# A hybrid attention and RWKV-7 layer on one Trainium2 core: scores in quarters of the array, a chain over two PSUM banks, a product that moves, and groups that start later

## Chip, core and metric

One core of a Trainium2 chip runs the whole layer in one launch. The metric is the device time of an execution in microseconds (us). Engines: TensorE (PE; its weight loads are listed as PEld), VectorE (DVE), ScalarE (ACT), GpSimd (POOL), SyncE (SP, which issues most DMAs). Each engine runs its own instructions in the order in which they were issued to it.

## The reference

`x` is 512 tokens of 1024 features, all fp32. 16 meta tokens are put ahead, so T = 528. After a layer norm, one product with `w_in` (1024 x 6656) gives everything that the two mixers need:

```python
q, k, v        # sliding-window attention: 16 query heads of 64, 2 key/value heads,
               # window 128, T5 relative bias, one sink a head
r, k, v, wl, al, gl = split(token_shift(z, mu))          # RWKV-7: 16 heads of 64
w = -softplus(-(w0 + tanh(wl) @ w2)) - 0.5;  decay = exp(-exp(w))
a = sigmoid(a0 + al @ a2);  g = sigmoid(gl) @ g2
kk = normalize(k * k_k);    k = k * (1 + (a - 1) * k_a)

def step(S, inp):                                        # S: 64 x 64 a head, T steps
    r_t, w_t, k_t, v_t, kk_t, a_t = inp
    sa = einsum('bhij,bhj->bhi', S, -kk_t)
    S = S * w_t + sa (x) (kk_t * a_t) + v_t (x) k_t      # outer products
    return S, einsum('bhij,bhj->bhi', S, r_t)

y = group_norm(y) * lnx_g + lnx_b
y = (y + sum(r * k * r_k) * v) * g                       # per head
```

The two results are merged by sigmoid gates, go through `w_out`, a residual and a layer norm, and then through an MLP of 4096 with squared ReLU and a second residual and norm.

## The kernel before

**Products in three.** An fp32 product is made of three matmuls on halves (`three`, L340 to L342): high by high, high by low, low by high. Weights arrive by DMA as `wraw` (128 x 1024, 512 KB), ACT casts the high half (`whi`, L256), DVE subtracts to get the low half (`wlo`, L259), one pair of instructions for each 512 columns. `hhi` and `hlo` are the halves of the normalized input, features on partitions. A *dense unit* is one 128-column tile of `w_in`: eight k steps of three matmuls, over two spans of 264 tokens (form 128x264) or, for queries and gates, one of 512 (128x512), into one of two banks `dps`.

**RWKV-7 in chunks.** The 16 heads go in 8 pairs, 128 partitions a pair, head 0 in rows 0 to 63 and head 1 in rows 64 to 127 (`ER`). The 512 tokens are 8 chunks of 64. For a pair:

- `rwkv_begin` and `rwkv_lora` (`llo`, L499; ACT `ta`, L500) make the decays. The evictions of the keys' unit (`k`) and the reads' unit (`r`) make the scaled vectors `BK` and `AX`; `rwkv_sums` takes norms (`ss`), DVE inverts them (`dv`). `rwkv_reads` runs when `r` is ready. It fills `AX` and then makes the product `rk` = r k r_k (L594), its high half `rkh` (ACT, L599) and low half `rkl` (DVE, L600).
- `rwkv_scores` (i = 0 and 1, four chunks each) multiplies `BK` (64 rows a head, 128 columns, one half for each kind of key) with `AX` (128 columns): eight matmuls `sc` (L668) a half, 64 rows by 128 columns, one bank a head. In a head's bank, the head's own 64 rows hold one kind of product, and the other 64 rows the other. Six DVE instructions take them out: `NT` (L676) twice and `GR` (L681) twice from the own rows, `AX` (L685) twice from the other rows.
- `rwkv_bonus` sums `rkh` and `rkl` over a head and multiplies with `v`; the result `bv` goes to memory and comes back as `bvm` for the output.
- The chunk's triangular matrix is inverted (`XB`, `X` L841, `up` L846, L822), then `rwkv_fold` (`wp` L873, `gq` L890) folds it into `AX`.
- `rwkv_chain` carries the state through the chunks in seven steps. A step is two matmuls `ch` (L948), head 0 into rows 0 to 63 and head 1 into rows 64 to 127 of one bank, eight steps side by side in it; then `follow` scales head 0's half on DVE (L906) and head 1's on ACT (L908) into `Z`, which the next step reads.
- `rwkv_outputs` (`Y`, L962), sums of squares (`grs`, with a power on POOL), `gyn`, `rwkv_norm`, then `z` (L1209, L1210), the gate, and the merge.

**Attention.** A query unit's eviction writes `qhi` (ACT, L1071) and `qlo` (DVE, L1072); four DMAs on SP (L1081) copy their halves to `qs0` and `qs1`, one tile a head. `qhi` lies in the tile with tag `sph`, of which there is one. `attention_scores` makes `sp` (L1136) in four parts, then `sb`, probabilities, transposes (`pt`, `pown`) and the outputs `o`. `turn_heads` (L1046) transposes the value heads (`vp`, L1052); it runs once for each of the two value heads.

**PSUM** has eight banks: two for `dps`, two with tag `g` (`sc`, `axt`, `gq`, `wp`, `bp`, `up`), two with tag `a` (`sp`, `vp`, `gp`, the lora's products, `ss`), one `ch` and one `Y`.

**What sets the order.** PE's order is written out by hand. The program goes through ten stages, s = -1 to 8. Stage s holds the inversion and chain of pair s - 1 (`solve`), the scores of pair s (`scan`), lora and norms of pair s + 1 (`project_in`), attention of pair s - 1, and the outputs and joins of pairs before. `weave` walks through a stage's list of steps, each with a start time, and puts k steps of the dense units between them until the sum of their estimated times reaches that start. The units of a stage come in this order: the RWKV gate and the attention gate of s - 1, the keys and reads of s + 1, the query of s, the values of s + 1. The instructions of the other engines come from the same functions; a scheduler sets their order by priorities (`PRI`), and the engines then run it in order. DMAs that SP issues stand in one queue in SP's order; weights are asked for two tiles ahead (L350).

The lines around the starts of the steps:

```python
            if s in (1, 5):
                items += [(8.6, (), turn_heads)]
            if 0 < s < PAIRS - 1:
                items += attend(s - 1, 9.2) + join(s - 1, 11.6, 25.4, 0)[:2]
```

Of the kernel before, what the change touches and what calls it, by code (L numbers as in the profile page):

```python
# [11 lines left out]
F32 = mybir.dt.float32  # L12
# [8 lines left out]
P = 128  # L21
# [7 lines left out]
HD = 64  # L29
# [101 lines left out]
def hybrid_layer_kernel(ctx: ExitStack, tc: tile.TileContext, I: dict, out: bass.AP):  # L131
# [454 lines left out]
    def rwkv_reads(j, r):  # L586
        S = SS[j]
        AXg = S["AX"].rearrange("p c k e t -> p e c k t")
        rx = c64(r)
        for e in range(2):  # L590
            R = slice(e * HD, (e + 1) * HD)
            dve.tensor_tensor(AXg[R, e, :, 1, :], rx[R], S["Px"][R, :, 1:], op=ALU.mult)
        rk = ew.tile([P, SEQ], F32, name="rk", tag="rk")
        dve.scalar_tensor_tensor(  # L594
            rk, r[:, NMETA:], vcol("r_k", j), S["kp"][:, NMETA:], op0=ALU.mult, op1=ALU.mult
        )
        rkh = ew.tile([P, SEQ], F32R, name="rkh", tag="rkh")
        rkl = ew.tile([P, SEQ], F32R, name="rkl", tag="u")
        act.copy(rkh, rk)  # L599
        dve.tensor_tensor(rkl, rk, rkh.bitcast(F32), op=ALU.subtract)  # L600
        S["rk"] = rkh, rkl
# [52 lines left out]
    def rwkv_scores(j, i):  # L654
        S = SS[j]
        if i == 0:
            S["NT"] = rw.tile([P, NCH, C], F32, name="NT", tag="NT", bufs=NBUF["NT"])
            S["GR"] = rw.tile([P, NCH, P], F32, name="GR", tag="GR", bufs=NBUF["GR"])
            S["Nd"] = dr.tile([BLKS], F32, name=f"Nd{j}")
        BK, dv, NT, GR, Nd = S["BK"], S["dv"], S["NT"], S["GR"], S["Nd"]  # L660
        AXg = S["AX"].rearrange("p c k e t -> p e c k t")
        msc = cv("msc")
        cs = slice(4 * i, 4 * i + 4)
        scs = [pg.tile([P, 512], F32, name="sc", tag="g") for e in range(2)]

        for c in range(4):
            for e in range(2):
                pe.matmul(  # L668
                    scs[e][:, c * P : (c + 1) * P], BK[ER[e], 4 * i + c, :],
                    AXg[ER[e], e, 4 * i + c], start=True, stop=True,  # L670
                )
        q4 = [ps.rearrange("p (c t) -> p c t", c=4) for ps in scs]
        with ahead(PRI["scores"]):
            for e in range(2):
                R = ER[e]
                dve.tensor_tensor(  # L676
                    NT[R, cs, :], q4[e][R, :, 0:C], B64(dv[R, cs], C), op=ALU.mult
                )
            for e in range(2):
                R, K_ = ER[e], ER[1 - e]  # L680
                dve.tensor_tensor(  # L681
                    GR[R, cs, C:P], q4[e][R, :, C:P],
                    msc[R, C:P].unsqueeze(1).to_broadcast([HD, 4, C]), op=ALU.mult,
                )
                dve.tensor_tensor(  # L685
                    AXg[K_, e, cs], q4[e][K_].rearrange("p c (k t) -> p c k t", k=2),
                    msc[K_].rearrange("p (k t) -> p k t", k=2).unsqueeze(1).to_broadcast(
                        [HD, 4, 2, C]
                    ), op=ALU.mult,
                )  # L690
        if i == 1:
            for e in range(2):
                nc.sync.dma_start(
                    blocks(Nd, 4 * e * BSTEP, [C, C], [8 * BSTEP, NCH], [1, C]), NT[ER[e]]
                )
# [204 lines left out]
    def follow(S, c, src, last):  # L900

        Z, PC = S["Z"], S["PC"]
        for e in range(2):
            dst, scale = Z[c][ER[e], e, :], PC[ER[e], last : last + 1]
            if e == 0:
                dve.tensor_scalar(dst, src[ER[e]], scale, None, op0=ALU.mult)  # L906
            else:
                act.activation(dst, src[ER[e]], AF.Copy, scale=scale)  # L908

    def rwkv_start(j, n):  # L910

        S = SS[j]
        if n == 0:
            S["meta"] = pch.tile([P, 512], F32, name="meta", tag="ch", bufs=PS[2])
            S["RHm"] = rw.tile([NMETA, 2, HD], F32, name="RHm", tag="RHm", bufs=2)
        ps, RHm = S["meta"], S["RHm"]
        p6 = [ps[:, q * C : (q + 1) * C] for q in range(6)]
        m = slice(0, NMETA)
        with ahead(PRI["start"]):
            if n == 0:  # L920
                for e in range(2):
                    pe.matmul(
                        p6[e][m], S["AKm"][:, e, :], S["SVm"][:, e, :], start=True, stop=True
                    )
                act.copy(RHm.rearrange("p e i -> p (e i)"), ps[m, 0 : 2 * C])
            if n == 1:
                for e in range(2):
                    pe.matmul(p6[2 + e][m], S["XTm"][:, e, :], RHm[:, e, :], start=True, stop=True)
                for e in range(2):
                    act.copy(S["SVm"][32 * e : 32 * e + NMETA, e, :], p6[2 + e][m])  # L930
            if n == 2:
                for e in range(2):
                    pe.matmul(
                        p6[4][ER[e]], S["BTm"][:, e, :], S["SVm"][:, e, :], start=True, stop=True
                    )
                follow(S, 0, p6[4], NCH)

    def rwkv_chain(j, c):

        S = SS[j]  # L940
        Z, GQ = S["Z"], S["AX"]
        if c == 0:
            ch = pch.tile([P, 512], F32, name="ch", tag="ch", bufs=PS[2])
            S["st"] = [ch[:, d * C : (d + 1) * C] for d in range(NCH)]
        st = S["st"]
        with ahead(PRI["chain"]):
            for e in range(2):
                pe.matmul(st[c][ER[e]], GQ[:, c, 0, e, :], Z[c][:, e, :], start=True, stop=True)  # L948
            follow(S, c + 1, st[c], c)

    def rwkv_outputs(j):
# [433 lines left out]
    def scan(j):  # L1385

        need = (f"k{j}", f"r{j}", f"v{j}")
        return [
            (0.0, need, F(rwkv_scores, j, 0)),
            (3.2, (), F(rwkv_meta, j)),  # L1390
            (3.2, (), F(rwkv_scores, j, 1)),
            (3.2, (), F(rwkv_inverse, j)),
            (5.6, (), F(rwkv_bonus, j)),
            (12.4, (), F(rwkv_turn_scores, j)),
            (18.6, (), F(rwkv_turn_keys, j)),
            (16.0, (), F(rwkv_inverse_place, j)),
            (23.2, (), F(rwkv_turn_values, j)),
        ]
# [45 lines left out]
    with tc.manual_schedule(engines={mybir.EngineType.PE}):  # L1444
        for s in range(-1, PAIRS + 1):
            if s <= PAIRS:
                units[:] = [u for u in all_units[: marks[s + 1]] if u[0] not in finished]
            items = []
            if s > 0:
                items += solve(s - 1)  # L1450
            if 0 <= s < PAIRS:
                items += scan(s)
            if s == -1:
                items += [
                    (0.0, (), F(rwkv_begin, 0)),
                    (9.0, ("wa",), F(rwkv_lora, 0, 0)),
                    (10.4, (), F(rwkv_lora, 0, 1)),
                    (20.0, ("k0",), F(rwkv_sums, 0)),
                ]
            if 0 <= s < PAIRS - 1:  # L1460
                items += project_in(s + 1)
            if s == 0:
                items += [(18.0, ("av",), F(aside_heads, 0))]
            if s == 4:
                items += [(26.0, (), F(aside_heads, 1))]
            if s in (1, 5):
                items += [(8.6, (), turn_heads)]
            if 0 < s < PAIRS - 1:
                items += attend(s - 1, 9.2) + join(s - 1, 11.6, 25.4, 0)[:2]
            if 1 < s < PAIRS:  # L1470

                items += attend_out(s - 2, 0.0, 4.6, 6.4) + join(s - 2, 0, 0, 7.0)[2:]
            if s == PAIRS - 1:
                items += [(10.0, (), merged_before)]
                items += attend(s - 1, 10.0) + attend_out(s - 1, 20.5, 22.9, 25.3)
                items += join(s - 1, 11.6, 26.5, 26.5)
                items += attend(s, 16.5)
                items += [(27.2, (), F(load_out, q, 0)) for q in range(3)]
            if s == PAIRS:
                items += attend_out(s - 1, 3.0, 5.4, 7.8) + join(s - 1, 0.0, 24.5, 25.5)  # L1480
                items += [(2.0, (), F(merged, s - 2)), (25.6, (), F(merged, s - 1))]
                items += [(3.0, (), residual_gain), (17.0, (), first_up)]
                items += [(3.0 + 3 * b, (), F(residual_rows, b)) for b in range(4)]
            weave(items, True)
# [262 lines left out]
```

## Time and profile before

| | us |
|---|---|
| median of 3 runs | 985.71 (983.71 to 985.78) |
| profiled execution, its own time | 984.06 |
| its span, first to last instruction | 982.3 |
| granted TensorE clock over the span | 0.997 of full |
| one inner stage, 165.0 to 228.5 | 63.5 |

"Busy" is the time in which an engine worked on an instruction, over the span. A row of a list of waits reads: engine, tile and line that waited, the engine, tile and line that it waited for, then the total in us, how often, and the longest. A timeline row reads: start, duration, engine, line, operation, tile written and tiles read, shapes, the count of like rows drawn together, and in brackets the idle time before it and what ended it. In a list of DMAs the last number is the median from issue to landing. An order row, further on, has no time: it is the line, the operation, output and inputs, and the shape.

### The profile page before, as it was taken

Reading aid. Unit: us, or ns where it says so; the run is one execution under the profiler, and the core shown is the slowest. Engines: PE = TensorE matmul, PEld = TensorE weight load, DVE = VectorE, ACT = ScalarE, POOL = GpSimd, SP = SyncE. Lnnn points to the kernel's source line nnn. Section 1 sums busy time; section 2 is a strip of 40 time slices with the busy share of each in tenths; the row PEclk is TensorE's granted clock in tenths of the full one; section 3 lists DMA queues with packets and bytes.
Section 4 is the critical chain, followed back from the end, with each engine's and each line's share of the span. In section 5 each row is a group of like instructions: output and inputs, shape, how many; then the busy total and the mean of one; then the engine's idle time right before and its main releaser. Section 6 shows DMA issues by size and latency. Waiting matters only on the chain.

```text
span 982.3 us, 19147 instructions
## 1 busy us (share of the span) xinstructions
PE 940.8 (96%) x7557; PEld 787.7 (80%) x7557; DVE 655.2 (67%) x1505; ACT 455.7 (46%) x1130; POOL 47.8 (5%) x108
## 2 busy tenths in 40 slices
PE   4989999999999999999998999999999999999996
PEld 3889878788887887887876778988888888888885
DVE  8677888877977788778876957566423244452427
ACT  6636457465474654745736724644321133432220
POOL 2001000010000100100001001000000000000001
PEclk9999999999999999999999999999999999999998
DMA  7546323223333332242434635133322323222222
GB/s 273 95 130 166 86 75 103 79 71 109 87 91 100 104 98 79 65 111 78 144 108 105 206 119 214 44 129 107 104 89 91 103 87 107 86 95 98 79 94 85
DMA packets 82674, 105.47 MB, mean 107 GB/s; under 512 B 47766, under 2 KB 54664, under 8 KB 82584
## 3 DMA queue, kind: packets, MB, share of 16 engines
q1 hardware_dynamic: 81088, 102.16, 34.3%
q10 hardware_dynamic: 1496, 2.08, 0.6%
q8 instruction: 59, 0.97, 0.4%
q14 instruction: 31, 0.25, 0.1%
HBM read 86.29 MB, written 13.74 MB: 102 GB/s over the span
## 4 chain that ended last, share of the span: by engine, by line
PE 72%; DVE 17%; ACT 4%; DMA 2%; issue 2%; POOL 2%; SPq 0%; DVEq 0%; ACTq 0%
PE dps L340 12%; PE dps L341 11%; PE dps L342 11%; PE acc L1516 6%; PE acc L1518 6%; PE acc L1517 6%; DVE wlo L259 3%; PE sc L668 2%; PE o L1290 1%; PE av L1194 1%; PE ch L948 1%; PE wp L873 1%; PE o L1291 1%; PE o L1292 1%; POOL grs L971 1%
## 5 line engine op out<-in xcount | busy, mean ns | idle before, releaser
L259 DVE TENSOR_TENSOR wlo<-wraw,whi 128x512 fp32r<-128x512 f32 x240 | 157.3, 686 | 168.3 <-ACT whi L256 167.6
L256 ACT CAST whi<-wraw 128x512 fp32r<-128x512 f32 x240 | 140.5, 617 | 266.3 <-PE dps L341 132.2
L340 PE MATMUL dps<-hhi,whi 128*128 128x264 f32 (+1 forms) x640 | 216.5, 338 | 4.5 <-DVE qlo L1072 2.8
L341 PE MATMUL dps<-hlo,whi 128*128 128x264 f32 (+1 forms) x640 | 203.5, 318 | 1.3 <-DVE hlo L321 1.3
L342 PE MATMUL dps<-hhi,wlo 128*128 128x264 f32 (+1 forms) x640 | 203.0, 317 | 0.4 <-DVE wlo L259 0.4
L340 PEld LDWEIGHTS dps<-hhi,whi 128*128 128x128 f32 x640 | 120.5, 188 | 19.4 <-DVE qlo L1072 4.1
L342 PEld LDWEIGHTS dps<-hhi,wlo 128*128 128x128 f32 x640 | 120.5, 188 | 9.0 <-DVE wlo L259 0.6
L341 PEld LDWEIGHTS dps<-hlo,whi 128*128 128x128 f32 x640 | 120.7, 189 | 7.5 <-DVE hlo L321 2.1
L341 PE MATMUL dps<-h1lo,whi 128*128 128x512 f32 (+1 forms) x256 | 97.5, 381 | 0.0
L340 PE MATMUL dps<-h1hi,whi 128*128 128x512 f32 (+1 forms) x256 | 97.5, 381 | 0.0
L342 PE MATMUL dps<-h1hi,wlo 128*128 128x512 f32 (+1 forms) x256 | 97.5, 381 | 0.0
L342 PEld LDWEIGHTS dps<-h1hi,wlo 128*128 128x128 f32 x256 | 48.1, 188 | 10.3
L341 PEld LDWEIGHTS dps<-h1lo,whi 128*128 128x128 f32 x256 | 48.1, 188 | 10.2
L340 PEld LDWEIGHTS dps<-h1hi,whi 128*128 128x128 f32 x256 | 48.1, 188 | 10.1
L1516 PE MATMUL acc<-whi,hhi 128*128 128x512 f32 x128 | 50.6, 395 | 0.0
L1517 PE MATMUL acc<-wlo,hhi 128*128 128x512 f32 x128 | 50.4, 394 | 0.0
L1518 PE MATMUL acc<-whi,hlo 128*128 128x512 f32 x128 | 50.2, 392 | 0.0
L1518 PE MATMUL acc<-whi,flo 128*128 128x512 f32 x112 | 44.1, 393 | 0.0
L1516 PE MATMUL acc<-whi,fhi 128*128 128x512 f32 x112 | 43.8, 391 | 0.0
L1517 PE MATMUL acc<-wlo,fhi 128*128 128x512 f32 x112 | 43.8, 391 | 0.0
L908 ACT ACTIVATE Z<-ch,PC 64x64 f32<-64x64 f32 x56 | 17.3, 310 | 36.4 <-DVE Z L906 35.7
L1616 DVE TENSOR_TENSOR rl<-rl 128x512 f32<-128x512 f32 (+1 forms) x36 | 22.8, 632 | 14.6 <-ACT hhi L1615 8.6
(302 smaller groups left out, 1732.7 us busy)
## 6 DMA issues: line engine op xcount, KB each, us to landing
wraw<-in_w_ff_dram SPq DMA_DIRECT2D x64, 512.0 KB, 3.6
wraw<-in_w_in_dram SPq DMA_DIRECT2D x52, 512.0 KB, 3.5
wraw<-in_w_out_dram SPq DMA_DIRECT2D x8, 512.0 KB
xt<-in_x_dram SPq DMA_DIRECT2D x4, 512.0 KB, 7.3
Nd<-NT SPq DMA_DIRECT2D x16, 128.0 KB, 2.9
bv<-bv SPq DMA_DIRECT2D x8, 256.0 KB, 2.1
bvm<-bv SPq DMA_DIRECT2D x8, 256.0 KB
qs<-qhi SPq DMA_DIRECT2D x16, 128.0 KB, 4.1
```

What stands on the lines that cost most here:

```text
L256: act.copy(hi[:n, qs], raw[:n, qs])
L259: dve.tensor_tensor(lo[:n, qs], raw[:n, qs], hi[:n, qs].bitcast(F32), op=ALU.subtract)
L340: pe.matmul(ps, whi, xhi, start=first, stop=False)
L341: pe.matmul(ps, whi, xlo, start=False, stop=False)
L342: pe.matmul(ps, wlo, xhi, start=False, stop=last)
L668: pe.matmul(scs[e][:, c * P : (c + 1) * P], BK[ER[e], 4 * i + c, :], AXg[ER[e], e, 4 * i + c], start=True, stop=True,)
L873: pe.matmul(w4[:, c, :], XB[:, 4 * i + c, :], S["AT"][:, 4 * i + c, :], start=True, stop=True,)
L908: act.activation(dst, src[ER[e]], AF.Copy, scale=scale)
L1516: pe.matmul(acc[b], xhi[k][:, bs], hi[:, ws], start=first, stop=False)
L1517: pe.matmul(acc[b], xhi[k][:, bs], lo[:, ws], start=False, stop=False)
L1518: pe.matmul(acc[b], xlo[k][:, bs], hi[:, ws], start=False, stop=last)
L1616: dve.tensor_tensor(r, r, r, op=ALU.mult)
```

## The change

Four edits, in one file.

1. **Scores in quarters.** Each matmul of `rwkv_scores` is split by output columns: 16 of 64 rows by 64 columns a half in place of 8 of 64 by 128. Head e's part d goes to bank d, rows `ER[e ^ d]`. So bank 0 holds the own rows of both heads, and bank 1 the other rows of both. `NT` and `GR` are taken out for both heads in one instruction each (128 partitions); `AX` still takes two. Four DVE instructions a half stand where six stood.
2. **Two banks for the chain.** Head 1's state goes to a second bank `ch2`, which has the tag `Y`, so it is the bank that `rwkv_outputs` writes after the chain. `follow` gets one source a head.
3. **The product moves.** `rk`, `rkh` and `rkl` leave `rwkv_reads` for a step of their own, `rwkv_products`, right after the first scores of the same pair in the next stage. `rk` moves from a tile of its own (tag `rk`, now `bv`'s alone) to the tag `sph`, where `qhi` lies; it can be written once `qhi`'s DMAs have read.
4. **Later starts.** `turn_heads` from 8.6 to 10.0, attention scores from 9.2 to 10.6, `gate_out` from 11.6 to 13.0, in stages 1 to 6 (`turn_heads` 1 and 5).

```diff
@@ rwkv_reads
-        rk = ew.tile([P, SEQ], F32, name="rk", tag="rk")
-        dve.scalar_tensor_tensor(
-            rk, r[:, NMETA:], vcol("r_k", j), S["kp"][:, NMETA:], op0=ALU.mult, op1=ALU.mult
-        )
+        S["r"] = r
+
+    def rwkv_products(j):
+
+        S = SS[j]
+
+        rk = at.tile([P, T], F32, name="rk", tag="sph")[:, :SEQ]
         rkh = ew.tile([P, SEQ], F32R, name="rkh", tag="rkh")
         rkl = ew.tile([P, SEQ], F32R, name="rkl", tag="u")
+        dve.scalar_tensor_tensor(
+            rk, S["r"][:, NMETA:], vcol("r_k", j), S["kp"][:, NMETA:], op0=ALU.mult, op1=ALU.mult
+        )
         act.copy(rkh, rk)
         dve.tensor_tensor(rkl, rk, rkh.bitcast(F32), op=ALU.subtract)
@@ rwkv_scores
-        scs = [pg.tile([P, 512], F32, name="sc", tag="g") for e in range(2)]
+        scs = [pg.tile([P, 512], F32, name="sc", tag="g") for d in range(2)]
         for c in range(4):
+            for d in range(2):
+                for e in range(2):
+                    to = ER[e ^ d]
+                    pe.matmul(
+                        scs[d][to, c * P : (c + 1) * P], BK[ER[e], 4 * i + c, to],
+                        AXg[ER[e], e, 4 * i + c], start=True, stop=True,
+                    )
+        own, other = (ps.rearrange("p (c t) -> p c t", c=4) for ps in scs)
+        with ahead(PRI["scores"]):
+            dve.tensor_tensor(NT[:, cs, :], own[:, :, 0:C], B64(dv[:, cs], C), op=ALU.mult)
+            dve.tensor_tensor(
+                GR[:, cs, C:P], own[:, :, C:P],
+                msc[:, C:P].unsqueeze(1).to_broadcast([P, 4, C]), op=ALU.mult,
+            )
             for e in range(2):
-                pe.matmul(
-                    scs[e][:, c * P : (c + 1) * P], BK[ER[e], 4 * i + c, :],
-                    AXg[ER[e], e, 4 * i + c], start=True, stop=True,
-                )
...
@@ follow, rwkv_chain
-                dve.tensor_scalar(dst, src[ER[e]], scale, None, op0=ALU.mult)
+                dve.tensor_scalar(dst, src[e][ER[e]], scale, None, op0=ALU.mult)
             else:
-                act.activation(dst, src[ER[e]], AF.Copy, scale=scale)
+                act.activation(dst, src[e][ER[e]], AF.Copy, scale=scale)
...
-            S["st"] = [ch[:, d * C : (d + 1) * C] for d in range(NCH)]
+            ch2 = pch.tile([P, 512], F32, name="ch2", tag="Y", bufs=PS[3])
+            S["st"] = [[b[:, d * C : (d + 1) * C] for b in (ch, ch2)] for d in range(NCH)]
...
-                pe.matmul(st[c][ER[e]], GQ[:, c, 0, e, :], Z[c][:, e, :], start=True, stop=True)
+                pe.matmul(st[c][e][ER[e]], GQ[:, c, 0, e, :], Z[c][:, e, :], start=True, stop=True)
@@ scan and the stages
             (0.0, need, F(rwkv_scores, j, 0)),
+            (0.0, (), F(rwkv_products, j)),
...
-                items += [(8.6, (), turn_heads)]
+                items += [(10.0, (), turn_heads)]
             if 0 < s < PAIRS - 1:
-                items += attend(s - 1, 9.2) + join(s - 1, 11.6, 25.4, 0)[:2]
+                items += attend(s - 1, 10.6) + join(s - 1, 13.0, 25.4, 0)[:2]
```

**How the orders move.** PE in stage 4, from the last matmul of the lora on; `dps` rows of form 128x512 are dense steps of a gate unit, in threes. Before:

```order
L499 MATMUL dps<-za,llo 128x264
L340 MATMUL dps<-hhi,whi 128x512
L341 MATMUL dps<-hlo,whi 128x512
L342 MATMUL dps<-hhi,wlo 128x512
L1136 MATMUL sp<-khi,qs_3935 128x256
L1137 MATMUL sp<-klo,qs_3935 128x256
...
L890 MATMUL gq<-GR,WT 128x128 x8
...
L948 MATMUL ch<-Z,AX 64x64 x2
```

With the change:

```order
L499 MATMUL dps<-za,llo 128x264
L340 MATMUL dps<-hhi,whi 128x512
L341 MATMUL dps<-hlo,whi 128x512
L342 MATMUL dps<-hhi,wlo 128x512
...
L895 MATMUL gq<-GR,WT 128x128 x8
L1143 MATMUL sp<-khi,qs_3980 128x256
L1144 MATMUL sp<-klo,qs_3980 128x256
...
L955 MATMUL ch<-Z,AX 64x64
L955 MATMUL ch_4520<-Z,AX 64x64
```

Before, one dense step (three matmuls) stands between `llo` and `sp`, and `gq` behind it; with the change three steps and `gq` stand between, and the chain's two matmuls write two tiles.

DVE from the end of stage 3 into stage 4, around the query's eviction `qlo`. Before:

```order
L592 TENSOR_TENSOR AX<-r,Px 64x8x64 x2
L594 SCALAR_TENSOR_TENSOR rk<-r,vc,kp 128x512
L1209 TENSOR_TENSOR z<-z,bvm 128x512
L1210 TENSOR_TENSOR z<-z,gg 128x512
L1072 SCALAR_TENSOR_TENSOR qlo<-dps,qhi 128x512
L259 TENSOR_TENSOR wlo<-wraw,whi 128x512 x2
L600 TENSOR_TENSOR rkl<-rk,rkh 128x512
L415 SCALAR_TENSOR_TENSOR v<-dps,vc,v 128x263
...
L676 TENSOR_TENSOR NT<-sc,dv 64x256 x2
L681 TENSOR_TENSOR GR<-sc,con 64x4x64
L685 TENSOR_TENSOR AX<-sc,con 64x8x64
...
L841 STREAM_TRANSPOSE X_4143<-XB 32x256 x2
```

With the change:

```order
L592 TENSOR_TENSOR AX<-r,Px 64x8x64 x2
L1216 TENSOR_TENSOR z<-z,bvm 128x512
L1217 TENSOR_TENSOR z<-z,gg 128x512
L259 TENSOR_TENSOR wlo<-wraw,whi 128x512 x2
L1079 SCALAR_TENSOR_TENSOR qlo<-dps,qhi 128x512
L259 TENSOR_TENSOR wlo<-wraw,whi 128x512
L415 SCALAR_TENSOR_TENSOR v<-dps,vc,v 128x263
L602 SCALAR_TENSOR_TENSOR rk<-r,vc,kp 128x512
...
L606 TENSOR_TENSOR rkl<-rk,rkh 128x512
L683 TENSOR_TENSOR NT<-sc,dv 128x256
L684 TENSOR_TENSOR GR<-sc,con 128x4x64
L690 TENSOR_TENSOR AX<-sc,con 64x8x64 x2
```

`rk` leaves its place ahead of `z` and stands behind `qlo`; two `wlo` come to stand ahead of `qlo`. Earlier on DVE, between `BKm` and `dv`, one `wlo` stands with the change where two stood.

SP's queue in the same place. Before:

```order
L1067 DMA bias<-tbd 128x2x128
L277 DMA wraw<-in_w_in_dram 128x1024 x2
L1204 DMA bvm<-bv_3429 128x512
L1081 DMA qs_3935<-qhi 64x512
L1081 DMA qs_3935<-qlo 64x512
```

With the change:

```order
L1074 DMA bias<-tbd 128x2x128
L277 DMA wraw<-in_w_in_dram 128x1024
L1211 DMA bvm<-bv_3479 128x512
L277 DMA wraw<-in_w_in_dram 128x1024
L1088 DMA qs_3980<-qhi 64x512
L1088 DMA qs_3980<-qlo 64x512
```

One weight load now stands behind `bvm` and next ahead of the copies of `qhi` and `qlo`.

More of the change, by code (lines that the diff above doesn't have):

```diff
@@ L663, in rwkv_scores @@
         cs = slice(4 * i, 4 * i + 4)
-        scs = [pg.tile([P, 512], F32, name="sc", tag="g") for e in range(2)]
+        scs = [pg.tile([P, 512], F32, name="sc", tag="g") for d in range(2)]
         for c in range(4):
-            for e in range(2):
-                pe.matmul(
-                    scs[e][:, c * P : (c + 1) * P], BK[ER[e], 4 * i + c, :],
-                    AXg[ER[e], e, 4 * i + c], start=True, stop=True,
-                )
[L672 to L675, printed above, removed]
-                dve.tensor_tensor(
[L677 to L686, printed above, removed]
+            for d in range(2):
[12 more added lines that the diff above has]
+            )
+            for e in range(2):
+                K_ = ER[1 - e]
+                dve.tensor_tensor(
+                    AXg[K_, e, cs], other[K_].rearrange("p c (k t) -> p c k t", k=2),
                     msc[K_].rearrange("p (k t) -> p k t", k=2).unsqueeze(1).to_broadcast(
@@ L935, in rwkv_start @@
                     )
-                follow(S, 0, p6[4], NCH)
+                follow(S, 0, (p6[4], p6[4]), NCH)
     def rwkv_chain(j, c):
```

## The prediction

> **What bounds it now.** I read the page's busy shares first, then TensorE's list of waits, the length of the eight-pair stages, and last the timeline around each wait.
>
> ```profile
> span 982.3 us, 19147 instructions
> PE 940.8 (96%) x7557; PEld 787.7 (80%) x7557; DVE 655.2 (67%) x1505; ACT 455.7 (46%) x1130; POOL 47.8 (5%) x108
> ```
>
> TensorE (PE) is busy 96% of the span, so only two things can move the end: its stalls, and a matmul group that changes its own length. The stalls, longest first (total us, times, longest):
>
> ```profile
> PE ch L948 <- ACT Z L908: 3.4, 5, 1.4
> PE dps L340 <- DVE qlo L1072: 2.8, 6, 0.5
> PE sp L1136 <- ACT ta L500: 2.7, 4, 0.7
> ...
> PE vp L1052 <- issue: 1.5, 1, 1.5
> PE vp L1052 <- ACT ta L500: 1.5, 1, 1.5
> ...
> PE sc L668 <- DVE AX L685: 1.0, 2, 0.6
> ```
>
> These, 12.9 us, are all that the change can reach. A stage (the work between two scans) shows the same; the columns are length, then busy us of PE, PEld, DVE, ACT, POOL:
>
> ```profile
> 165.00:228.50 63.50, 62.38 (x686) 53.27 (x686) 52.00 (x140) 36.86 (x105) 4.22 (x10) 1.00 0.33 91
> 355.30:420.70 65.40, 62.78 (x689) 53.64 (x689) 52.61 (x141) 37.10 (x107) 4.23 (x9) 1.00 0.31 85
> ```
>
> About 1 us of 63.5 is idle, and 2.6 in the stage that also turns the value heads. DVE is busy 52 of 63.5 us, off the path on average, but some stretches of it are solid.
>
> **Later groups.** In scan 4 the attention scores wait for a bank that ScalarE (ACT) frees:
>
> ```profile
> 318.31 0.63 ACT L514 ACTIVATE iP<-L 128x528 f32<-128x528 f32 x1
> 318.49 0.40 PE L342 MATMUL dps<-hhi,wlo 128*128 128x512 f32 x1
> ...
> 319.03 0.84 ACT L500 ACTIVATE ta<-dps,drv 128x264 f32<-128x264 f32 x2
> 319.56 0.39 PE L1136 MATMUL sp<-khi,qs 128*128 128x256 f32 x1 [0.67 <-ACT ta L500]
> ```
>
> A 512-column matmul steps on every 0.24 us, so `sp` could have begun at 318.73 and is 0.83 late. In the new order six more such matmuls (1.4 us) and the `gq` group (1.09, row below) stand ahead of it: its turn comes at 318.73 + 2.5 = 321.2, after both `ta` (319.87). Nothing is left: 4 x 0.83 = -3.3.
>
> In scans 1 and 5 `vp` is first in the line:
>
> ```profile
> 126.09 0.28 PE L499 MATMUL dps<-za,llo 128*128 128x264 f32 x1
> 127.27 0.84 ACT L500 ACTIVATE ta<-dps,drv 128x264 f32<-128x264 f32 x2
> 127.84 0.49 PE L1052 MATMUL vp<-con,vT 64*128 64x64 f32 x5 [1.47 <-issue]
> ```
>
> It starts 1.75 after the last `llo`, which alone would take 0.12: 1.63 lost. Six dense matmuls now fill 1.4 of that and the switch of form 0.1: 0.1 to 0.2 is left. 2 x 1.5 = -3.0. Bounds for both: the whole -6.6, or nothing if ACT gets later by as much; no ACT instruction moves ahead of `ta`, so I take -6.3. The steps moved issue no DMA.
>
> **Two banks for the chain.** ACT's half of a step waits for DVE's, though the matmul is long done:
>
> ```profile
> 393.63 0.27 DVE L906 TENSOR_SCALAR Z<-ch,PC 64x64 f32<-64x64 f32 x1
> 393.93 0.31 ACT L908 ACTIVATE Z<-ch,PC 64x64 f32<-64x64 f32 x1 [1.16 <-DVE Z L906]
> 394.29 0.34 PE L948 MATMUL ch<-Z,AX 128*64 128x64 f32 x4 [0.64 <-ACT Z L908]
>   DVE Z L906: 35.7, 36
> ```
>
> With a bank per head ACT goes at once and PE waits for DVE alone, so each stalled step gains ACT's 0.31. Of the five (0.46, 0.64, 0.60, 0.24, 1.44 idle) three gain 0.3, the fourth its 0.24, the last about 0.65 (there ACT is behind a cast and a gate as well, and only the gate changes places): -1.8. The second bank is `Y`'s, so `Y` now waits for ACT's last `Z`:
>
> ```profile
> 335.99 0.31 ACT L908 ACTIVATE Z<-ch,PC 64x64 f32<-64x64 f32 x1
> 336.79 1.15 PE L962 MATMUL Y<-Z,AX 128*64 128x64 f32 x32
> ```
>
> That ends 0.49 before its turn: nothing. But the scores' evictions (five DVE instructions of 0.41 after each first pair) are now behind the first chain steps instead of ahead. In scan 4 I count DVE at 329.4 to 330.0 with the third `Z`, and PE wanting it at 329.75: 0.2 a stage in five stages, +1.0. Sum -0.8; bounds -3.4 (all five gone) and +3 (0.8 in six stages, less the 1.8).
>
> **Products out of the reads.** What `qlo` waits for, at the end of stage 3:
>
> ```profile
> 285.18 1.29 DVE L259 TENSOR_TENSOR wlo<-wraw,whi 128x512 fp32r<-128x512 f32 x2
> ...
> 288.61 0.75 DVE L594 SCALAR_TENSOR_TENSOR rk<-r,vc,kp 128x512 f32<-128x512 f32 x1
> 289.28 0.69 DVE L1209 TENSOR_TENSOR z<-z,bvm 128x512 f32<-128x512 f32 x1
> 290.00 0.69 DVE L1210 TENSOR_TENSOR z<-z,gg 128x512 f32<-128x512 f32 x1
> 290.67 0.69 DVE L1072 SCALAR_TENSOR_TENSOR qlo<-dps,qhi 128x512 fp32r<-128x512 f32 x1
> ...
> 290.65 0.28 PE L342 MATMUL dps<-hhi,wlo 128*128 128x264 f32 x1
> 291.42 0.39 PE L340 MATMUL dps<-hhi,whi 128*128 128x264 f32 x1 [0.49 <-DVE qlo L1072]
> ```
>
> DVE is solid from `gyn` to `qlo`, so what counts is how much stands between. `rk` (0.75) leaves. But two `wlo` now stand between `z` and `qlo`, and only one where two stood at 285.18: one more in all, 0.65. Net -0.1 of a loss of 0.77 - 0.12 = 0.65, six times: -0.6. Bounds: -3.9 if the wait goes, +3.9 if a whole further `wlo` (0.65) comes between. ACT's `qhi` gets earlier (it waits no more for `rkh`), but DVE, not ACT, is last.
>
> The stall of `rk` goes to the next stage. There it has a new wait, in a tile that it shares with `qhi`: the DMAs that copy `qhi` out.
>
> ```profile
> qs<-qhi SPq DMA_DIRECT2D x16, 128.0 KB, 4.1
> 295.20 0.69 DVE L259 TENSOR_TENSOR wlo<-wraw,whi 128x512 fp32r<-128x512 f32 x1 [1.63 <-ACT whi L256]
> ...
> 300.49 0.89 DVE L841 STREAM_TRANSPOSE X<-XB 32x256 f32<-32x256 f32 x2
> ...
> 301.80 0.69 PE L846 MATMUL up<-X,NT 32*32 32x32 f32 x32
> 291.99 0.56 SPq L1081 DMA_DIRECT2D qs<-qhi  x1
> ```
>
> The last copy of `qhi` is issued at 291.99 and lands, by 2.4 (`qlo`'s median on this list) to 4.1 us, at 294.4 to 296.1; a weight load of 512 KB now goes ahead of it on SP's queue, so I take 295.2. Behind `rk` on DVE stand `wlo`, two evictions of `v`, `wlo`, `rkl`, the scores' evictions, `pown` and `X`, and PE waits for `X` at `up`, with 0.42 to spare (301.38 to 301.80). `rk` fills what was idle until 295.20, then runs 0.75 over; `rkl` adds 0.69; the evictions give back 0.84 (below). X is 0.6 late, PE 0.15: seven stages, +1.0. Bounds: 0 (landing by 294.4) and 0.9 more a stage, +7.
>
> At the start ACT no longer holds weight casts behind `rkh`: -0.3 of a stall of 1.1 (bounds 0 and -1.1).
>
> **Scores in quarters.** PE goes from 8 matmuls of 64 rows by 128 columns to 16 of 64 by 64.
>
> ```profile
> 295.61 1.09 PE sc L668 x16
> 310.82 1.78 PE wp L873 x16
> 294.56 0.73 PE L822 MATMUL up<-X,NT 16*32 16x16 f32 x64
> L681 DVE TENSOR_TENSOR GR<-sc,con 64x256 f32<-64x256 f32 x32 | 13.4, 418 | 0.4
> ```
>
> Eight full-array matmuls of 128 moving columns (`wp`) take 1.78; eight half-height ones (`sc`) 1.09, so two run side by side. Four side by side would again take 1.09. `up` is the nearest: 32 matmuls on four row tiles, 16 moving columns each, one bank. One after another at `wp`'s pace they would take 32 x 16 x 1.78 / 1024 = 0.89; they hold PE for 0.66 (294.56 to the next group at 295.22). So tiles in one bank do overlap. I take 0; bounds 0 and, two at a time, 1.78 - 1.09 = 0.69 each, 16 x 0.69 = +11.0. [...]
>
> DVE saves one `NT` (0.42) and one `GR` (0.42) per half, 16 x 0.84 = 13.4 us, hidden beside PE, except that the second scores of scan 0 wait for them: -0.2 of the 1.0. If PE stopped covering DVE, the 13.4 would count.
>
> **Sum.** -6.3 - 0.8 - 0.6 + 1.0 - 0.3 - 0.2 = -7.2. The profiled execution took 984.06 (span 982.3 and 1.8 around it): 976.9. The median of the runs is 985.71, 1.65 above it: 978.5. I forecast 977.5, in between.
>
> **Rivals.** *Quarters two at a time*: decided by whether a pair of row tiles may fill one bank; +11.0 gives 988.5, slower than before. [...] 0.09. *The products hold DVE*: copies land at 296.1, PE loses 0.95 more per stage than I took, 977.5 + 6.6 = 984.1, no change; for it the 4.1, against it the 2.4. 0.10. *The chain inherits the wait*: the score evictions make two steps late by 0.4 in six stages, 977.5 + 4.8 - 1.0 = 981.3; for it DVE's 52 us, against it three stages whose chain never waited. 0.13. *The wait at `qlo` goes too*: if DVE's backlog shrinks by one instruction, 977.5 - 3.3 = 974.2. 0.13.
>
> **Numbers.** My forecast has 0.55, its own range 973.5 to 981. The range of all, 970 to 985.5, leaves out the slow rival and the far ends. 0.2% (2 us) is what a measurement can tell from no change: faster are the forecast, the chain and `qlo`, 0.81, less 0.01 for a forecast that misses far: 0.80; the same are the held DVE and that 0.01: 0.11; slower the quarters: 0.09.
>
> **What would show it.** `sp` and `vp` leave TensorE's waits; ACT's `Z` no longer waits for DVE's; `qlo` stays with 0.5 each; `up` after `X` appears with 0.1 to 0.2; a `sc` group keeps 1.09. A `sc` group of 1.8, or `X` with 1 us a stage, makes me wrong.

## The result

| | before | with the change |
|---|---|---|
| median of 6 runs, us | 985.75 (983.71 to 987.50) | 996.56 (991.46 to 999.19) |
| ratio, 95% interval | | 1.010 (1.0081 to 1.0119) |
| profiled execution, us | 984.06 | 996.61 |
| its span, us | 982.3 | 994.8 |
| granted TensorE clock over the span | 0.997 | 0.985 |

The change makes the kernel 1.0% slower, 11 us over the upper end of the range that was forecast. From the page of the changed kernel: the span, the busy row and the row of the granted clock (40 slices, tenths; the two 8s in the middle are new).

```profile
span 994.8 us, 19604 instructions
PE 952.3 (96%) x7813; PEld 794.1 (80%) x7813; DVE 642.4 (65%) x1473; ACT 454.6 (46%) x1130; POOL 46.0 (5%) x108
PEclk9999999999999999989989999999999999999998
```

DVE has 12.8 us less to do, and TensorE is "busy" 11.5 us longer with the same products. Its own list of waits, and the row for `rk` from the whole list (total us, times, longest):

```profile
DVE rk L602 <- DMA qs<-qhi: 29.2, 6, 6.2
PE up L851 <- DVE X L846: 10.5, 11, 3.0
PE sp L1143 <- DVE sb L1146: 2.3, 2, 2.1
PE dps L340 <- DVE qlo L1079: 1.9, 6, 0.3
```

`sp` for `ta` and `vp` are gone, as forecast, and so is `ch` for `Z`, of which only a part was forecast to go. In their place TensorE waits 10.5 us for `X`, which waits behind `rk`. The end of stage 3 in the changed kernel, the same place that the prediction shows of before:

```profile
290.25 0.33 SPq L1211 DMA_DIRECT2D bvm<-bv  x1
291.58 0.33 SPq L277 DMA_DIRECT2D wraw<-in_w_in_dram  x1
292.36 0.51 SPq L1088 DMA_DIRECT2D qs<-qhi  x1
292.98 0.53 SPq L1088 DMA_DIRECT2D qs<-qlo  x1
293.60 0.55 SPq L1088 DMA_DIRECT2D qs<-qhi  x1
...
293.27 0.48 DVE L415 SCALAR_TENSOR_TENSOR v<-dps,vc,v 128x263 f32<-128x263 f32 x1
298.87 0.75 DVE L602 SCALAR_TENSOR_TENSOR rk<-r,vc,kp 128x512 f32<-128x512 f32 x1 [5.12 <-DMA qs<-qhi]
...
304.55 0.89 DVE L846 STREAM_TRANSPOSE X<-XB 32x256 f32<-32x256 f32 x2
305.12 0.22 PE L851 MATMUL up<-X,NT 32*32 32x32 f32 x2 [1.91 <-DVE X L846]
```

The second copy of `qhi` is issued at 293.60 and has landed when `rk` starts, at 298.87. DVE stands still for 5.1 us, all that is queued behind `rk` moves back, and TensorE is idle for 1.9 us. What follows that idle is in the table by stretches of one microsecond (PE, PEld, DVE, ACT, POOL, then the granted clock, the DMA share and GB/s):

```profile
304.00:305.00 1.00, 0.00 (x0) 0.00 (x0) 0.97 (x3) 0.00 (x0) 0.00 (x0) 1.00 0.06 25
305.00:306.00 1.00, 0.72 (x32) 0.64 (x32) 0.43 (x1) 0.00 (x0) 0.00 (x0) 1.00 0.00 0
306.00:307.00 1.00, 1.00 (x21) 0.60 (x15) 0.41 (x3) 0.72 (x2) 0.30 (x2) 0.70 0.08 16
307.00:308.00 1.00, 1.00 (x15) 0.70 (x16) 0.68 (x5) 0.49 (x3) 0.01 (x1) 0.50 0.00 0
308.00:309.00 1.00, 1.00 (x26) 0.89 (x20) 0.00 (x0) 0.23 (x2) 0.00 (x0) 0.50 0.03 2
309.00:310.00 1.00, 1.00 (x10) 0.69 (x3) 0.68 (x2) 0.00 (x0) 0.00 (x0) 0.59 0.00 0
```

The clock is halved for 3.4 us, which loses 1.7 us of work. Such tables behind the six idles before `up` show losses of 1.7, 0, 1.7, 0, 3.4 and 3.4 (after idles of 1.84, 0.25, 1.91, 1.04, 1.71 and 2.98), 10.2 us together; 1.7 more are lost near 28 us.

**The account**, by TensorE's pace (start to start, less what the matmuls take), from stalls of 0.4 us or more: `sp` -3.4, `vp` -3.3, chain -4.2, `qlo` -1.7, second scores and the start -1.2, last stage +1.4, `X` +10.8. Together -1.6. The clock adds 11.9. That makes +10.3 of the 12.5 between the spans; the other 2.2 are in smaller pieces that I did not follow.

### The profile page after: what moved, and what is told of

Same layout as the page of the kernel before. It is cut to its first block, busy times and chain, and to the rows that moved or that the text cites. A ratio compares the mean times of both kernels' runs of the same rounds, so it can differ in the third digit from the quotient of the medians.

```text
span 994.8 us, 19604 instructions
## 1 busy us (share of the span) xinstructions
PE 952.3 (96%) x7813; PEld 794.1 (80%) x7813; DVE 642.4 (65%) x1473; ACT 454.6 (46%) x1130; POOL 46.0 (5%) x108
## 4 chain that ended last, share of the span: by engine, by line
PE 73%; DVE 14%; DMA 4%; ACT 4%; issue 2%; POOL 1%; SPq 0%; DVEq 0%; ACTq 0%; POOLq 0%
PE dps L340 13%; PE dps L341 11%; PE dps L342 11%; PE acc L1524 6%; PE acc L1526 6%; PE acc L1525 6%; DVE wlo L259 3%; DMA qs<-qhi 2%; PE gq L895 2%; PE sc L677 2%; PE o L1297 1%; PE av L1201 1%; PE wp L878 1%; PE ch L955 1%; PE o L1298 1%
## 5 line engine op out<-in xcount | busy, mean ns | idle before, releaser
L342 PEld LDWEIGHTS dps<-h1hi,wlo 128*128 128x128 f32 x256 | 48.1, 188 | 10.2
L340 PEld LDWEIGHTS dps<-h1hi,whi 128*128 128x128 f32 x256 | 48.1, 188 | 10.2
L341 PEld LDWEIGHTS dps<-h1lo,whi 128*128 128x128 f32 x256 | 48.1, 188 | 10.2
```

The source lines that it names most:

```text
L340: pe.matmul(ps, whi, xhi, start=first, stop=False)
L341: pe.matmul(ps, whi, xlo, start=False, stop=False)
L342: pe.matmul(ps, wlo, xhi, start=False, stop=last)
```

## Experiments

Every run is compared with the kernel before on the same chip; those three groups of runs had medians of 985.68, 986.42 and 986.15 for it.

### One part alone, and one part undone

**`own_tile`**, the change with one line back:

```diff
-        rk = at.tile([P, T], F32, name="rk", tag="sph")[:, :SEQ]
+        rk = ew.tile([P, SEQ], F32, name="rk", tag="rk")
```

> The change with one thing undone: rk keeps a tile of its own and shares none with qhi, so it no longer waits for the copies of qhi. Theory A (the shared tile: in the changed kernel rk waits 29.2 us for the copies, X comes late, TensorE idles 10.5 us before up, and the granted clock halves after four of these idles, 10.2 us more): the waits of up are under 1 us in sum, the granted clock is back at 0.997, and the waits at sp, vp and the chain (3.3 + 3.3 + 4.2) stay away. rk and rkl now stand ahead of qlo on DVE, with one weight split less, which makes qlo up to 0.7 later in six stages. 985.7 - 10.8 + 4.2 = 979, between 974 and 981. Theory B (the quarters of the scores or the later groups cost the time, by more matmuls and a lower clock): it stays at 993 to 997, with a clock under 0.99.

Measured 980.5, ratio 0.9953 (0.9936 to 0.9971), clock 0.995. `up` has no wait for `X` left, and `qlo`'s has grown. The order on DVE and TensorE's waits:

```profile
286.07 0.75 DVE L602 SCALAR_TENSOR_TENSOR rk<-r,vc,kp 128x512 f32<-128x512 f32 x1
286.73 0.69 DVE L1217 TENSOR_TENSOR z<-z,gg 128x512 f32<-128x512 f32 x1
287.33 0.69 DVE L259 TENSOR_TENSOR wlo<-wraw,whi 128x512 fp32r<-128x512 f32 x1
287.93 0.69 DVE L606 TENSOR_TENSOR rkl<-rk,rkh 128x512 fp32r<-128x512 f32 x1
288.65 0.69 DVE L1079 SCALAR_TENSOR_TENSOR qlo<-dps,qhi 128x512 fp32r<-128x512 f32 x1
...
PE dps L340 <- DVE qlo L1079: 5.9, 6, 1.0
```

Theory A holds: one shared tile makes 16 us between the medians, 1.5% between the two ratios. The second lesson is that `rk` goes back ahead of `qlo` as soon as it may. In the changed kernel it is the shared tile alone that keeps it behind.

**`products_only`**, the kernel before with `rwkv_products` and the shared tile.

> The kernel before with the product moved into the tile of the queries, and nothing else of the change. Theory A: rk waits for the copies as in the whole change, up waits for X by about 10 us in sum, and the clock drops after the idles over 1.7 us: 985.7 + 10 to 21 = 996 to 1007, without the gains of the other parts. Theory B: rk's wait is hidden, 984 to 987.

Measured 988.75, ratio 1.0028 (1.0010 to 1.0046). Slower, but by 3 us, not by 10 to 21: the tile alone is not enough. Here `rk` waits 9.5 us in all, and TensorE 1.8 for `X`:

```profile
287.68 0.35 SPq L277 DMA_DIRECT2D wraw<-in_w_in_dram  x1
290.51 0.33 SPq L1210 DMA_DIRECT2D bvm<-bv  x1
290.94 1.15 SPq L1087 DMA_DIRECT2D qs<-qhi  x2
...
295.14 0.75 DVE L602 SCALAR_TENSOR_TENSOR rk<-r,vc,kp 128x512 f32<-128x512 f32 x1 [1.73 <-DMA qs<-qhi]
...
  DMA qs<-qhi: 9.5, 6
...
PE up L852 <- DVE X L847: 1.8, 4, 1.3
```

The weight load went out 3.3 us ahead of the copies, and both copies of `qhi` go first; in the whole change the load goes out 0.8 us ahead. The later copy of `qhi` takes 3.6 us from issue (291.55, the second of the two drawn together) to `rk`, in the whole change 5.3. Over the six stages in which `rk` waits for it, that is 2.4 to 4.8, 3.3 on average, and in the whole change 4.1 to 6.5, 5.2 on average. The packets of the DMAs, by size, show what goes on in this stage (2 KB: `bvm` and the copies; 4 KB: weights; other sizes left out):

```
             2 KB packets start    4 KB packets start
products     291.5 to 295.1        288.7 to 290.6, then from 294.9
whole        291.2 to 292.4,       292.6 to 295.8 (120 of 128 by 294.8), then from 296.5
             294.1 to 298.1
```

With the part alone the load is through before the copies begin, and the next load begins as they end. In the whole change 107 of the load's 128 packets start ahead of the first of the copies' 256, which starts 1.7 us after the first copy was issued, and the copies' last 31 start among the packets of the next load. The 16 DMA engines are busy 0.83 to 1.00 of each microsecond from 293 to 298.

**`later_only`**, the kernel before with the three later starts.

> The kernel before with the later starts alone. Theory A: the waits of sp for ta (4 x 0.85) and of vp (2 x 1.64) go, and nothing takes their place: 985.7 - 6.6 = 979, between 977.5 and 981; the chain's waits stay. Theory B: 986 or more, with a wait that is as long at another place.

Measured 987.84, ratio 1.0019 (1.0005 to 1.0032): my theory falls. `sp` and `vp` wait no more, but:

```profile
PE ch L948 <- ACT Z L908: 6.6, 12, 1.4
PE dps L340 <- DVE qlo L1072: 4.9, 6, 0.8
```

The chain waits twelve times in place of five, because the scores and their evictions now lie between its steps, and `qlo` waits 0.8 in place of 0.5. The wait had only moved.

**`chain_only`**, the kernel before with the second bank.

> The kernel before with the second bank for the chain alone. Theory A: the five waits of ch for ACT's Z (4.2 us over the pace of the matmuls) go altogether, since in the whole change none is left: 985.7 - 4.2 = 981.5, between 980.5 and 984. The prediction's own term, 0.3 a wait and 1.0 given back, would be 984.9. A rival: DVE's Z takes the place of ACT's, and nothing changes.

Measured 986.94, ratio 1.0014 (0.9996 to 1.0031). The five waits of the chain shrink to two of 0.3, and `qlo` takes it back:

```profile
PE dps L340 <- DVE qlo L1074: 5.5, 6, 0.9
PE sp L1138 <- ACT ta L500: 2.7, 4, 0.7
```

**`quarters_only`**, the kernel before with the new `rwkv_scores`.

> The kernel before with the scores in quarters alone. Theory A (a group keeps its length, as 1.10 to 1.09 in the whole change; two DVE instructions less a half are hidden): 985.7 - 0.2 = 985.5, between 984 and 987. Rival of the prediction (two at a time): +11, 996. A third way, as for the later groups and the second bank: the order on DVE shifts, and a wait at qlo grows, up to +2.

Measured 985.20, ratio 0.9974 (0.9959 to 0.9988): a gain, a little more than expected. The two-at-a-time rival is out. A group in the changed kernel, at full clock and at half:

```profile
296.93 1.10 PE L677 MATMUL sc<-AX,BK 64*64 64x128 f32 x32
...
307.30 1.99 PE L677 MATMUL sc<-AX,BK 64*64 64x128 f32 x32
```

1.10 where the eight larger matmuls took 1.09: so four quarters run side by side, two in each bank.

**`all_but_products`**, the change without its third part.

> The change without the third part: later starts, the second bank and the quarters together, and the product where it was. Theory A (the parts need one another: the later starts put the chain's waits up, 12 in place of 5, and the second bank takes them away; both put qlo later): sp, vp and the chain no longer wait, qlo waits about 1.1 a stage since rk and two splits stand ahead of it: 986 - 10.8 + 6 x 0.5 = 978, between 976.5 and 981. If the parts only add up (+2.1, +1.0 and -1 of the three runs alone), 988.

Measured 981.99, ratio 0.9950 (0.9931 to 0.9969). The three parts, +0.19%, +0.14% and -0.26% alone, make -0.5% together: the later starts put waits on the chain that the second bank takes away, and no wait of `ch` for `Z` is left here. What is left is `qlo`, 6.1 us, and with it the time is 1 us above the range expected. The interval of `own_tile` is nearly the same, so these runs show no gain from moving the product once `rk` may run ahead of `qlo` again.

### The idle and the clock

**`fillers`**, the change with

```diff
+                for _ in range(16):
+                    pe.matmul(up[:, 256:512], hhi[:, 0, 0:P], hhi[:, 1, 0:256], start=True, stop=True)
```

ahead of the matmuls that read `X` (`up` lies in the bank of `Y`).

> The change with 16 matmuls of no use (128x256, into a place of the up bank that is written anew behind them) ahead of the third group of up in each of the eight pairs, so that TensorE works while it waits for X. They take 16 x 0.11 = 1.8 us. rk's wait stays. Theory A (the idle before up is what halves the granted clock, for 3.41 or 6.83 us at a time, 10.2 us lost in all): the clock is back at 0.997; the fillers cost 2.0 in the two stages whose idle was shorter, and 1.8 each in the two pairs without it: 996.6 - 10.2 + 5.6 = 992, between 989 and 995. Rival (the clock falls for another reason, as the matmuls on small tiles behind): it stays at 0.985, 996.6 + 5.6 = 1002.

Measured 992.44 (expected 992), ratio 1.0057 (1.0036 to 1.0079). It does 16 us of useless work (eight groups of 2.0) and is 4 us faster than the change itself. Its stretch behind the same group, and the changed kernel's:

```profile
303.00:309.00 6.00, 6.00 (x100) 5.02 (x97) 3.76 (x11) 2.79 (x11) 0.32 (x2) 1.00 0.21 75
```

```profile
303.00:309.00 6.00, 3.93 (x76) 2.83 (x75) 3.48 (x11) 1.44 (x5) 0.31 (x2) 0.78 0.18 64
```

`rk` still waits (26.5 us in all), the same small tiles run behind, and the clock stays whole behind `up`. In all ten runs it was 0.995 to 0.998, in the six of the change 0.985 to 0.991. So it is the idle that halves the clock.

How long an idle must be has no sharp answer in these traces. From 60 to 600 us of all fourteen profiles, an idle of TensorE of 1.6 us or more was followed by the half clock 9 times of 14, one of 1.05 to 1.6 us 8 times of 28, one of 0.7 to 1.05 never. But the length of one idle is not all: two more half-clock stretches, at 72.8 in `later_only` and at 77.0 in `before_loads_first`, came behind two idles of 0.54 to 0.58 us a microsecond apart. The same wait of `vp`, 1.47 us, cost nothing in the kernel before, and 1.7 us of clock both times in `quarters_only`, which may be one reason why these runs spread. The half-clock stretches behind `up` in the changed kernel lasted 3.4 us twice (losses of 1.7) and 6.8 us twice (losses of 3.4). The shortest single idle with the half clock behind it was 1.12 us (`loads_first`, at 369).

### The copies

**`hi_first`**, the change with the two loops around the copies exchanged, so that both copies of `qhi` go first.

> The change with the four copies of a query in another order: both of qhi, then both of qlo, on the same queue. rk waits for the later copy of qhi. In the whole change that one is issued at 293.60, behind one of qlo, and lands at 298.8; now it is issued 0.6 earlier. Theory A1 (what counts is the place in the queue): it lands 0.6 or more earlier, X is as much earlier in six stages, -3.6, and the idle before up is short enough in three of the four stages that the clock is not halved there, -7: 996.6 - 10.6 = 986, between 983 and 991. Theory A2 (what counts is that the 16 DMA engines are full with the weight load ahead, busy share 0.83 to 1.00 from 293 to 298): it lands as late as before, 995 to 998.

Measured 992.2 (986.05 to 997.19 in eleven of the twelve runs), ratio 1.0054 (1.0031 to 1.0076), between the two. `rk` waits 26.2 us in place of 29.2, 0.5 a stage, as the place in the queue would have it; the later copy still takes 4.4 us in this stage, 5.5 on average over the six. And `up` waits 8.1 in place of 10.5. The profiled run was the fastest of the twelve, and in it the clock stayed whole behind `up`, after idles of up to 1.9. That was luck: the clocks of the other ten are 0.986 to 0.995.

**`copies_by_act`**, the change with

```diff
-                    nc.sync.dma_start(
+                    (nc.scalar if d == 0 else nc.sync).dma_start(
```

and the loops exchanged.

> The change with the two copies of qhi issued by ScalarE, which has written qhi, in place of SP; those of qlo stay on SP. They no longer stand behind the weight load and the copy of qlo. Theory A: they are issued at about 291 in the time of the fourth stage and land by 294, where DVE has come to rk; its wait is under 0.5 a stage, X is in time, the clock is 0.997, and what the other parts gain is left: 985.7 - 10.8 (sp, vp, chain) - 1.0 (qlo) = 974, between 971 and 978. Rival: the issues (1.1 us on ScalarE a stage) hold back the weight casts, and the time is 979 or more.

Measured 979.94, ratio 0.9935 (0.9912 to 0.9959): clearly faster than both kernels, with the ratio of `own_tile` inside its interval, though 2 us above the range expected. And not by the way I gave:

```profile
287.98 1.12 ACTq L1088 DMA_DIRECT2D qs<-qhi  x2
288.91 0.33 SPq L277 DMA_DIRECT2D wraw<-in_w_in_dram  x1
...
294.27 0.75 DVE L602 SCALAR_TENSOR_TENSOR rk<-r,vc,kp 128x512 f32<-128x512 f32 x1 [3.18 <-DMA qs<-qhi]
...
PE up L851 <- DVE X L846: 4.4, 8, 1.5
```

The copies are issued before the load, from another queue, and the later one still takes 5.6 us on average from issue to `rk`. `rk` waits 3.0 a stage, not 0.5. The gain comes from the earlier issue; the landing itself is no shorter, with a load right behind the copies in place of one ahead. That this load is what slows them here was not tested by itself. TensorE's waits for weight splits are 1.2 us in all there, as in the whole change, so the rival, which would show there, is out.

**`loads_first`**, the change with `'load': 300` in the scheduler's table.

> The change with one constant more: weight loads and splits get 300 in place of 100 in the scheduler's table of priorities. In the order, the weight load that was next ahead of the copies of qhi and qlo goes back ahead of bvm, both copies of qhi come ahead of those of qlo, and one weight split in place of two stands between z and qlo. rk keeps the shared tile. Theory A (the copies land late because their packets go through the same 16 DMA engines as 512 KB of weights that were issued just ahead): the copies land in about 3 us, as with the product alone (291.5 to 295.3, no packet of a load among them), rk waits under 2 us a stage, X costs TensorE under 2 in sum, the clock is at 0.997: 986 - 10.8 - 1 = 974, between 972 and 978. Rival (the copies are slow whatever stands ahead, or the order of the rest decides): rk waits over 3 us a stage, 988 or more.

**`before_loads_first`**, its control.

> The kernel before with the loads' priority at 300, a control. rk has a tile of its own there and no copy is waited for, so by theory A the place of the loads is worth nothing: 986, between 984.5 and 987.5. If it gains 5 or more, what loads_first gains is not the copies' landing.

Measured 986.94, ratio 1.0004 (0.9989 to 1.0020), and for the control 991.76, ratio 1.0059 (1.0037 to 1.0082). Both times were missed, but the waits went as theory A has it:

```profile
288.19 0.34 SPq L277 DMA_DIRECT2D wraw<-in_w_in_dram  x1
...
294.15 1.15 SPq L1088 DMA_DIRECT2D qs<-qhi  x2
...
297.21 0.75 DVE L602 SCALAR_TENSOR_TENSOR rk<-r,vc,kp 128x512 f32<-128x512 f32 x1 [1.04 <-DMA qs<-qhi]
...
  DMA qs<-qhi: 9.7, 6
...
PE up L851 <- DVE X L846: 1.7, 4, 1.1
```

With the load 6 us ahead, `rk` waits 9.7 us in place of 29.2, in the same tile, and `X` costs 1.7. The later copy takes 3.0 us on average from issue to `rk`, in place of 5.2; that both copies of `qhi` now go first is no reason for it, since with that alone (`hi_first`) it took 5.5. So the load beside the copies is the larger part of what makes them late. It is not all: in four stages the copy took about 2.4 us, but in two, at 168 and 358, 3.8 and 4.7 with the load as far ahead, and why stays open. The time is another matter. The constant puts weight splits ahead of the first layer norm, so `tm` waits as it did not before (row of the control), and both kernels come at 62.7 and 62.9 us to the place where the kernel before is at 58.4. Against its control `loads_first` gains 4.8 us. Of the 12 that I expected, `qlo` takes 2.9 (4.8 us of wait in place of 1.9) and `X` 1.7; the rest is open.

```profile
PE tm L290 <- DVE xm L241: 4.0, 1, 4.0
```

**`own_tile_loads_first`**, both edits.

> The change with rk in a tile of its own and the loads' priority at 300. On DVE now rk and one weight split stand between AX and qlo, and rkl behind qlo; with the own tile alone rk, a split and rkl did. By theory A only qlo's wait changes, 1.15 a stage there, by one DVE instruction of 0.69: 980.2 - 6 x 0.6 = 976.5, between 975 and 979. If it stays at 980, qlo is not set by what stands ahead of it on DVE.

Measured 985.06, ratio 0.9991 (0.9976 to 1.0005): missed. It bears the same late start, 6.7 us better than the control. `qlo`'s stall went from 1.15 to 1.01 a stage, not to 0.5. The fourth stage shows why one instruction less on DVE brought so little: counted from the start of TensorE's last matmul ahead of the stall, DVE came to the first `z` at -2.1 us (291.22, 293.32) where with the own tile alone it came at -2.7 (285.46, 288.13). The 0.6 saved behind that place was lost ahead of it; by what, I did not follow.

## Why the prediction was wrong

**Later groups, -6.3: right in the whole change, wrong by itself.** The waits went, by 6.7. That nothing would take their place is true only with the second bank (`later_only`).

**Two banks, -0.8: too small.** All five waits went, 4.2. The +1.0 for evictions ahead of the third `Z` did not appear: no wait of `ch` is left in the changed kernel.

**`qlo`, -0.6: about right.** A stall of 0.65 became 0.49, six times, and TensorE's wait at 94 us for another tile of DVE (`ftmp`) went as well: -1.7 together.

**Quarters, 0 and -0.2: right in kind.** 1.10 for 1.09, with two row tiles of 64 in each bank. The rival's +11.0, a group of 1.78 at full clock, no run shows. The gain by itself is 0.26%, more than the 0.2 us.

**The product in the next stage, +1.0: this is the step that failed.** I wrote that the last copy "is issued at 291.99 and lands, by 2.4 (...) to 4.1 us, at 294.4 to 296.1", and took 295.2, that is 3.2 us from its issue. To compare that with the changed kernel, the two timelines must be laid together. Its `up` group at this place, on TensorE, starts 1.39 us later than that of before, which the prediction shows at 294.56:

```profile
295.95 0.72 PE L827 MATMUL up<-X,NT 16*32 16x16 f32 x64
```

Less these 1.39, the copy was issued at 292.2, nearly where I had it, although two weight splits stand ahead of `qlo` and a load ahead of the copies. But `rk` could start only at 297.5, 5.3 us after the issue. So the landing was the term that was mis-sized: 3.2 taken, 5.3 measured here, 4.1 to 6.5 over the six stages. I took the middle of landing times read from the old order, in which the last load had gone out 4.2 us ahead of the first copy, and I named the load that now goes next ahead of them without a price of its own. At the rate of the fullest microsecond here its 512 KB take 1.5 us of all 16 engines, which the copies need as well: from 296.1 to 296.4, with no packet of a load under way, the 16 engines were busy 0.93 (the last number of the row is GB/s):

```profile
293.00:294.00 1.00, 1.00 (x9) 1.00 (x9) 0.75 (x2) 0.05 (x1) 0.00 (x0) 1.00 0.98 344
```

With 297.5 in the prediction's own sum, `rk` runs 2.3 later, and `X` costs TensorE not 0.15 but up to 2.4 in this stage, where 1.9 of idle were measured. Over the six stages it is 10.8, beyond the bound of 7, which stopped at a landing of 4.1.

**The clock, not in the sum at all: +11.9.** Each long idle was priced at its length. Of those the change made, four were followed by 1.7 or 3.4 us more. The rival "the products hold DVE" was the mechanism, with 0.10 and 984.1. It is 12 us too low as well: its copies land at 296.1, and it has no clock in its price either.

## What to carry to other kernels

A tile that is shared with the source of a DMA takes the DMA's landing time into an engine's queue (`rk` waited 29.2 us in all here): price it with the landing beside the loads of the new order (5.2 us on average here), not with the median of the old one. Before times of two kernels are compared, lay their timelines together at one instruction that both have. Price an idle of TensorE over a microsecond at its length plus the chance of a halved clock behind it (here 17 of 42 idles of 1.05 us or more, with 1.7 or 3.4 us lost behind each of four in the changed kernel); work of no use in the gap can be cheaper than the gap (`fillers`, 992.44 us, against 996.56). Edits that move waits along one chain are to be tried together: here two that gain nothing alone gain, with a small third, half a per cent.

## What the runs showed of the hardware

That the granted clock can halve behind a single idle of 1.12 us (`loads_first`, at 369), or behind two of 0.54 to 0.58 us a microsecond apart (`later_only`, at 72.8, and `before_loads_first`, at 77.0), in some cases and not in others (17 of 42 idles of 1.05 us or more), for 3.4 us or twice that (the change). And that a copy of 64 rows by 2 KB within the chip landed, by the start of `rk` that waits for it, about 2.4 us after its issue in four of six stages when the last load had gone out 6 us ahead of the first copy (`loads_first`; 3.8 and 4.7 in the other two), 2.4 to 4.8 with a load 3.3 us ahead (`products_only`), and 4.1 to 6.5 with one close by: 0.4 to 0.8 us ahead in the same queue (the change, `hi_first`) or 0.9 us behind from another (`copies_by_act`).
